# Strassen pairs for 24 of 32 down products of layer 1's MLP

## The chip, the cores and the metric

One Trainium2 chip, of which this kernel uses one core. The metric is the device time of one execution in microseconds. The core's engines run side by side, each with its own instructions in a fixed order: TensorE (PE) multiplies matrices, VectorE (DVE), ScalarE (ACT) and GpSimd (POOL) work element by element, SyncE (SP) issues the transfers between device memory and on-chip memory. They wait for one another through semaphores.

## The reference

A model of two layers over 1,040 tokens (16 learned ones ahead of 1,024 of the input), width 1,024, all in fp32. Each layer is a mixer (layer 0: stick-breaking attention beside an S5 state space; layer 1: a gated delta net) and an MLP, each with a norm before and after it and a residual. Only layer 1's MLP is touched:

```python
def sq_relu_mlp(h, w1, w2):
    return jnp.square(jax.nn.relu(h @ w1)) @ w2
...
        hn = rms_norm(hs, pre_mlp_norm[i])
        hs = hs + rms_norm(sq_relu_mlp(hn, mlp_w1[i], mlp_w2[i]), post_mlp_norm[i])
    return hs[:, N_META:]
```

`w1` is 1024 x 4096 and `w2` 4096 x 1024. Layer 1's MLP runs over the last 1,024 tokens alone, since only they are returned.

## The kernel before

Activations lie transposed: features on the 128 partitions, tokens along the row. A product in fp32 accuracy is three matmuls. Each operand is split into a high part (`split` and `weight` cast it on ACT into `hh` or `whi`) and a low part (what is left, a subtraction on DVE or POOL into `hl` or `wlo`); then high x high, high x low and low x high are added up in one PSUM bank. With 512 token columns that is three matmuls of 128 x 128 by 512.

The MLP (`mlp`) first makes the 4,096 hidden features in 32 tiles of 128 (up), then multiplies them with `w2` (down).

Up: tiles 0 to 5 plainly; tiles 6 to 31 in 13 pairs (`pair`) by Strassen's algorithm in Winograd's form, which multiplies 2 x 2 blocks with seven products in place of eight. The blocks are two hidden tiles by two halves of 512 tokens (tokens 16 to 527 and 528 to 1039). `ops` makes the weight sums of a pair on POOL (lines 451 to 459) and its seven split operands (line 440). Each product is 12 matmuls, and DVE adds the results up (line 487). `block` applies the square ReLU: on DVE a `scalar_tensor_tensor` with the row scale `rb` (line 491), on ACT the square (line 415). Each of the four finished blocks is stored by SP to a buffer in device memory, `hd` (line 416).

Down: `down([2g, 2g+1])` for 14 groups of two hidden tiles, then `down([28, 29, 30, 31], True)`, whose chunks are 384, 384 and 256 columns and with which the norm and the output go. `hidden(k)` loads one tile of activations (`hr`, or `wraw` for the first four), splits it, the low part on POOL (line 229). `weight` loads 128 x 1024 of `w2` into `wraw`, casts on ACT (line 163), makes the low part on POOL (line 166). For each of eight output tiles and two halves PE adds up both hidden tiles (six matmuls, lines 176 to 178), and DVE copies (line 552) or adds (line 554) the bank to `acc`.

The order of work on each engine is that in which the code is written, unless a scheduler of the framework moves it: instructions of one engine are put in order ahead of time, by when it expects operands and buffers. Buffers are rings: `wraw` has two tiles, `whi` and `wlo` four each, `slot` shares 33 tiles among many names. A write into a ring's tile waits until the last reader of what lay there is done.

Of the kernel before, what the change touches and what calls it, by code (L numbers as in the profile page):

```python
# [11 lines left out]
F32 = mybir.dt.float32  # L12
F32R = mybir.dt.float32r
BF16 = mybir.dt.bfloat16
I32 = mybir.dt.int32
AF = mybir.ActivationFunctionType
# [30 lines left out]
def f(ap):  # L47
    return ap.bitcast(F32)


class Net:
# [349 lines left out]
    def mlp(self, layer, st, hs_d, chunks, gpre, ahead=None):  # L401

        nc = self.nc
        w1, w2 = self.io["w1"], self.io["w2"]
        hd = self.dr.tile([128, 32, NT], F32, tag="hd%d" % layer, name="hd", bufs=1)
        hid = {}
        t0, h = (0, 520) if layer == 0 else (16, 512)
        half = ((0, 260), (260, 260)) if layer == 0 else ((0, 512),)
        wide = chunks if layer == 0 else CH4
# [3 lines left out]
        def put(m, o, n, x):  # L413

            nc.scalar.activation(x[:, :n], x[:, :n], AF.Square)
            nc.sync.dma_start(hd[:, m, o:o + n], x[:, :n])
# [13 lines left out]
        bank = cycle((self.mm, self.tr, self.mm, self.tr, self.mm, self.tr, self.ax))  # L430
# [12 lines left out]
        def ops(ma, mb):  # L443

            ra, rb = self.raw(), self.raw()
            nc.sync.dma_start(ra[:, :1024], w1[layer, ma])
            nc.sync.dma_start(rb[:, :1024], w1[layer, mb])
            a11, a12, a21, a22 = ra[:, :512], ra[:, 512:1024], rb[:, :512], rb[:, 512:1024]
            S = [self.sp.tile([128, 520], F32, tag="sS", name="sS", bufs=4)[:, :512] for _ in range(4)]
            o = [operand(a11)]  # L450
            nc.gpsimd.tensor_add(S[0], a21, a22)
            nc.gpsimd.tensor_sub(S[1], S[0], a11)
            o.append(operand(S[1]))
            o.append(operand(a12))
            nc.gpsimd.tensor_sub(S[2], a11, a21)
            o.append(operand(S[2]))
            o.append(operand(a22))
            o.append(operand(S[0]))
            nc.gpsimd.tensor_sub(S[3], a12, S[1])
            o.append(operand(S[3]))  # L460
            return o

        def pair(ma, mb, T):

            A11, S2, A12, S3, A22, S1, S4 = ops(ma, mb)
            B11 = lambda k: (st["hi"][k][:, t0:t0 + h], st["lo"][k][:, t0:t0 + h])
            B21 = lambda k: (st["hi"][k + 4][:, t0:t0 + h], st["lo"][k + 4][:, t0:t0 + h])
            B22 = lambda k: (st["hi"][k + 4][:, t0 + h:t0 + 2 * h], st["lo"][k + 4][:, t0 + h:t0 + 2 * h])
            T1, T3 = (lambda k: tuple(x[:, :h] for x in T[k][0])), (lambda k: tuple(x[:, h:2 * h] for x in T[k][0]))
            T4, T2 = (lambda k: tuple(x[:, :h] for x in T[k][1])), (lambda k: tuple(x[:, h:2 * h] for x in T[k][1]))  # L470

            def product(A, B, then):
                for c, (o, n) in enumerate(half):
                    pt = next(bank)()[:, :n]
                    for i in range(4):
                        wh, wl = (w[:, i * 128:(i + 1) * 128] for w in A)
                        bh, bl = B(i)
                        nc.tensor.matmul(pt, wh, bh[:, o:o + n], start=i == 0, stop=False)  # L478
                        nc.tensor.matmul(pt, wh, bl[:, o:o + n], start=False, stop=False)  # L479
                        nc.tensor.matmul(pt, wl, bh[:, o:o + n], start=False, stop=i == 3)  # L480
                    then(c, o, n, pt)

            P, U, R, Q = {}, {}, {}, {}

            def total(x, name, n, *ab):
                x = self.tmp(name) if x is None else x
                nc.vector.tensor_add(x[:, :n], *ab)
                return x

            def block(m, o, n, x):  # L490
                nc.vector.scalar_tensor_tensor(x[:, :n], x[:, :n], 0.0, st["rb"][:, o:o + n], op0=ALU.max, op1=ALU.mult)
                put(m, o, n, x)

            def p1(c, o, n, pt):
                P[c] = self.tmp("p1")
                nc.scalar.copy(P[c][:, :n], pt)

            def p2(c, o, n, pt):
                block(ma, t0 + o, n, total(P[c], "", n, pt, P[c][:, :n]))

            def p6(c, o, n, pt):
                U[c] = total(None, "u2", n, pt, P[c][:, :n])

            def p7(c, o, n, pt):
                R[c] = total(None, "u3", n, pt, U[c][:, :n])

            def p4(c, o, n, pt):
                block(mb, t0 + o, n, total(None, "c21", n, pt, R[c][:, :n]))

            def p5(c, o, n, pt):  # L510
                Q[c] = total(U[c], "", n, pt, U[c][:, :n])
                block(mb, t0 + h + o, n, total(R[c], "", n, pt, R[c][:, :n]))

            def p3(c, o, n, pt):
                block(ma, t0 + h + o, n, total(Q[c], "", n, pt, Q[c][:, :n]))

            product(A11, B11, p1)
            product(S2, T2, p6)
            product(A12, B21, p2)
            product(S3, T3, p7)  # L520
            product(A22, T4, p4)
            product(S1, T1, p5)
            product(S4, B22, p3)

        def hidden(k):

            raw = self.raw() if k < 4 else self.slot("hr")
            hi, lo = self.slot("hh", F32R), self.slot("hl", F32R)
            nc.sync.dma_start(raw[:, t0:NT], hd[:, k, t0:NT])
            self.split(hi[:, t0:NT], lo[:, t0:NT], raw[:, t0:NT], lo_eng=nc.gpsimd)  # L530
            hid[k] = (hi, lo)

        def down(ks, last=False):
            first = ks[0] == 0
            for k in ks:
                hidden(k)
            W = {k: self.weight(w2[layer, k], act=True) for k in ks}
            out, hook, ch = None, None, wide
            if last:
                ch = chunks  # L540
                if ahead is None:
                    ch = CH3
                if ahead is not None:
                    ahead()
                ssq = self.slot("ssq_o")
                reuse = [t for k in ks for t in hid[k]]
                *out, hook = self.residual(acc, ssq, reuse, G_POSTMLP + 8 * layer, hs_d, gpre, ch)

            def ev(m, c, pt):
                o, n = ch[c]  # L550
                if first:
                    nc.vector.tensor_copy(acc[m][:, o:o + n], pt)
                else:
                    nc.vector.tensor_add(acc[m][:, o:o + n], pt, acc[m][:, o:o + n])  # L554
                if last:
                    self.sq_acc(ssq, m, m == 0, acc[m][:, o:o + n], o, n)

            self.gemm(range(8), ks, lambda m, k: tuple(w[:, m * 128:(m + 1) * 128] for w in W[k]), lambda k: hid[k], ch, "c" if last else "m", ev, hook, None if last else six)
            for k in ks:
                del hid[k]  # L560
            return out
# [4 lines left out]
            up([m], "m")  # L566
        for m in range(UPC, 32, 2):
            pair(m, m + 1, T)
        acc = [self.slot("acc") for _ in range(8)]
        for g in range(14):  # L570
            down([2 * g, 2 * g + 1])
        return down([28, 29, 30, 31], True)


    def exp_exact(self, out, x):
# [1248 lines left out]


NSLOT, NTMP, AHEAD, UPC = 33, 10, 4, 6
ROW, RP, R0 = 1, 5, 2
FA, FB = 14, 14
RM = 4
# [315 lines left out]
```

## Time and profile before

| | |
|---|---|
| median of 3 runs | 2947.3 us (2946.3 to 2951.14) |
| the profiled execution | 2945.58 us |
| its span, first to last instruction | 2943.5 us |
| mean granted TensorE clock | 0.944 |
| TensorE busy in the span | 2767.2 us (94%), 16488 instructions recorded |
| VectorE busy | 1752.0 us (60%) |
| POOL busy | 1305.4 us (44%) |
| ScalarE busy | 1063.4 us (36%) |

Times in the trace count from the span's start. Layer 1's up pairs lie at about 2293 to 2564 us, the first down matmul at 2564.29 us, the last group of four from about 2873 us. In a row of a stage stand the stretch, its length, then for each engine busy microseconds and in brackets the instructions, then the granted clock (1.00 is full), the mean share of the DMA engines that were busy, and what they moved. In a row of the order of time stand start, length, engine, line, operation, and in square brackets how long the engine had been idle and who ended that.

### The profile page before, as it was taken

Reading aid. Unit: us, or ns where it says so; the run is one execution under the profiler, and the core shown is the slowest. Engines: PE = TensorE matmul, PEld = TensorE weight load, DVE = VectorE, ACT = ScalarE, POOL = GpSimd, SP = SyncE. Lnnn points to the kernel's source line nnn. Section 1 sums busy time; section 2 is a strip of 40 time slices with the busy share of each in tenths; the row PEclk is TensorE's granted clock in tenths of the full one; section 3 lists DMA queues with packets and bytes.
Section 4 is the critical chain, followed back from the end, with each engine's and each line's share of the span. In section 5 each row is a group of like instructions: output and inputs, shape, how many; then the busy total and the mean of one; then the engine's idle time right before and its main releaser. Section 6 shows DMA issues by size and latency. Waiting matters only on the chain. (4 is left out here: it accounts for less than half of the span.)

```text
span 2943.5 us, 44168 instructions
## 1 busy us (share of the span) xinstructions
PE 2767.2 (94%) x16488; PEld 2505.5 (85%) x16488; DVE 1752.0 (60%) x3107; ACT 1063.4 (36%) x2108; POOL 1305.4 (44%) x942
## 2 busy tenths in 40 slices
PE   7899999899999999999897978999998999999997
PEld 7689667788999999999886977899898888888887
DVE  8642768666755555555746896544538545444445
ACT  4111656554533332110446322443435433322101
POOL 5552324325577766342522123111135777664423
PEclk9989667889999999999998988999999999999998
DMA  3435212124433343221426667444334333442322
GB/s 129 157 122 157 80 57 80 48 87 167 133 112 114 111 146 136 95 80 54 135 90 214 198 204 230 126 139 141 121 105 153 118 113 104 135 155 94 107 88 70
DMA packets 209766, 360.99 MB, mean 123 GB/s; under 512 B 45488, under 2 KB 131200, under 8 KB 209552
## 3 DMA queue, kind: packets, MB, share of 16 engines
q1 hardware_dynamic: 205664, 353.49, 37.2%
q10 hardware_dynamic: 3888, 4.69, 0.4%
q8 instruction: 130, 2.13, 0.3%
q14 instruction: 84, 0.69, 0.1%
HBM read 247.07 MB, written 111.03 MB: 122 GB/s over the span
## 5 line engine op out<-in xcount | busy, mean ns | idle before, releaser
L166 POOL TENSOR_TENSOR wlo<-wraw,whi 128x1024 fp32r<-128x1024 f32 x129 | 315.2, 2456 | 764.6 <-ACT whi L163 272.7
L176 PE MATMUL mm<-ahi,whi 128*128 128x344 f32 (+2 forms) x1200 | 418.0, 349 | 41.3 <-DVE cx L1333 28.8
L178 PE MATMUL mm<-ahi,wlo 128*128 128x344 f32 (+2 forms) x1200 | 400.3, 334 | 2.3 <-DVE wlo L166 2.3
L177 PE MATMUL mm<-hl,whi 128*128 128x352 f32 (+4 forms) x1136 | 388.0, 342 | 0.0
L554 DVE TENSOR_TENSOR acc<-mm,acc 128x344 f32<-128x344 f32 (+4 forms) x308 | 177.3, 576 | 179.1 <-PE mm L178 179.1
L176 PEld LDWEIGHTS mm<-ahi,whi 128*128 128x128 f32 x1200 | 235.6, 196 | 49.6 <-DVE cx L1333 30.3
L178 PE MATMUL mm<-hh,wlo 128*128 128x352 f32 (+4 forms) x752 | 260.4, 347 | 5.0 <-POOL wlo L166 5.0
L176 PE MATMUL mm<-hh,whi 128*128 128x352 f32 (+4 forms) x752 | 260.2, 346 | 0.6 <-DVE acc L554 0.6
L178 PEld LDWEIGHTS mm<-ahi,wlo 128*128 128x128 f32 x1200 | 235.5, 196 | 4.3 <-DVE wlo L166 3.2
L554 DVE TENSOR_TENSOR acc<-tr,acc 128x344 f32<-128x344 f32 (+2 forms) x260 | 152.9, 588 | 139.7 <-PE tr L178 139.7
L177 PEld LDWEIGHTS mm<-hl,whi 128*128 128x128 f32 x1136 | 218.1, 192 | 11.2 <-issue 0.4
L163 ACT CAST whi<-wraw 128x1024 fp32r<-128x1024 f32 x77 | 77.6, 1045 | 351.7 <-PE tr L177 326.9
L178 PE MATMUL tr<-hh,wlo 128*128 128x512 f32 (+2 forms) x560 | 196.1, 350 | 0.0
L177 PE MATMUL tr<-hl,whi 128*128 128x512 f32 (+2 forms) x560 | 195.9, 350 | 0.0
L176 PE MATMUL tr<-hh,whi 128*128 128x512 f32 (+2 forms) x560 | 195.8, 350 | 0.0
L229 POOL TENSOR_TENSOR hl<-hr,hh 128x1040 fp32r<-128x1040 f32 (+1 forms) x56 | 135.6, 2429 | 78.0 <-ACT hh L228 62.3
L178 PEld LDWEIGHTS mm<-hh,wlo 128*128 128x128 f32 x752 | 143.1, 191 | 16.5 <-POOL wlo L166 6.2
L176 PEld LDWEIGHTS mm<-hh,whi 128*128 128x128 f32 x752 | 143.0, 190 | 10.9 <-DVE acc L554 0.9
L440 POOL TENSOR_TENSOR wlo<-sS,whi 128x512 fp32r<-128x512 f32 x104 | 143.4, 1381 | 14.1 <-ACT whi L439 14.0
L366 POOL TENSOR_TENSOR ssq_o<-ssq_o,sq 128x344 f32<-128x344 f32 (+4 forms) x84 | 93.9, 1117 | 79.8 <-ACT sq L365 79.3
L177 PE MATMUL mm<-hh,whi 128*128 128x344 f32 (+2 forms) x384 | 128.6, 335 | 0.0
L244 POOL TENSOR_TENSOR ssq<-ssq,sq 128x344 f32<-128x344 f32 (+2 forms) x84 | 90.6, 1079 | 84.9 <-ACT sq L243 76.8
(528 smaller groups left out, 7788.0 us busy)
## 6 DMA issues: line engine op xcount, KB each, us to landing
wraw<-w SPq DMA_DIRECT2D x128, 512.0 KB, 3.6
wraw<-wino SPq DMA_DIRECT2D x32, 512.0 KB, 5.2
hr<-hd SPq DMA_DIRECT2D x28, 520.0 KB, 5.6
hr<-hd SPq DMA_DIRECT2D x28, 512.0 KB, 4.5
dm<-dmd SPq DMA_DIRECT2D x16, 520.0 KB, 5.1
hsd<-hs SPq DMA_DIRECT2D x48, 172.0 KB, 1.9
hd<-u SPq DMA_DIRECT2D x52, 130.0 KB, 2.1
hd<-u SPq DMA_DIRECT2D x26, 256.0 KB, 2.0
```

The source lines that it names most:

```text
L163: nc.scalar.copy(hi[:, :n], raw[:, :n])
L166: (nc.vector if fast else nc.gpsimd).tensor_sub(lo[:, :n], raw[:, :n], f(hi[:, :n]))
L176: nc.tensor.matmul(pt, wh, h[:, o:o + n], start=i == 0, stop=False)
L177: nc.tensor.matmul(pt, wh, l[:, o:o + n], start=False, stop=False)
L178: nc.tensor.matmul(pt, wl, h[:, o:o + n], start=False, stop=i == len(kts) - 1)
L229: (lo_eng or nc.vector).tensor_sub(lo, src, f(hi))
L244: nc.gpsimd.tensor_add(st["ssq"][:, o:o + n], st["ssq"][:, o:o + n], sq[:, :n])
L366: nc.gpsimd.tensor_add(ssq[:, o:o + n], ssq[:, o:o + n], sq[:, :n])
L440: nc.gpsimd.tensor_sub(lo, src, f(hi))
L554: nc.vector.tensor_add(acc[m][:, o:o + n], pt, acc[m][:, o:o + n])
```

## The change

In layer 1 (`SD = (1,)`), hidden tiles 6 to 29 (`ND = 12` pairs) go through the down product in six groups of two pairs, by Strassen's algorithm as well: the blocks are now two hidden tiles by two token halves on one side, and two hidden tiles by two halves of the 1,024 output features on the other.

In the up pairs DVE makes four sums of the finished activation blocks (`sums`), and SP stores seven blocks per pair to a new buffer `ht` in place of four to `hd`.

`down_pairs(g, X)` goes through seven products, b = 0, 2, 4, 5, 3, 1, 6. For each it loads the activation blocks of two pairs into a raw weight tile (`raw()`, line 589), splits them with the low part on DVE (line 229), and multiplies by a weight block of both pairs: the quarters of `w2` are loaded in halves of 256 KB (`w2r`, line 568), and POOL makes the sums, S1 in a tile of its own (line 574) and three differences in place (line 579). The cast is on ACT (line 594), the low weights on POOL (line 595). Each product is 24 matmuls, four PSUM banks, which DVE copies (line 609, first group) or adds (line 611) to the seven sums `X`. `down([0, 1], X=X)` starts `acc` from its products and four of those sums (line 650), `combine(X)` adds the rest on DVE and POOL (lines 618 to 624), then follow `down([2, 3])` and `down([4, 5, 30, 31], True)`. On TensorE 14,788 rows become 14,644.

```diff
+SD, ND = (1,), 12
...
             def block(m, o, n, x):
                 nc.vector.scalar_tensor_tensor(x[:, :n], x[:, :n], 0.0, st["rb"][:, o:o + n], op0=ALU.max, op1=ALU.mult)
-                put(m, o, n, x)
+                if not seven:
+                    put(m, o, n, x)
+                    return
+                nc.scalar.activation(x[:, :n], x[:, :n], AF.Square)
...
+            def sums(o, n):
+
+                a, b, c, d = (H[k + (o,)][:, :n] for k in ((0, 0), (0, 1), (1, 0), (1, 1)))
+                ta, tb, tc = self.tmp("ta"), self.tmp("tb"), self.tmp("tc")
+                nc.vector.tensor_sub(ta[:, :n], b, a)
+                nc.vector.tensor_sub(b, d, b)
+                nc.vector.tensor_sub(tb[:, :n], d, ta[:, :n])
+                nc.vector.tensor_sub(tc[:, :n], c, tb[:, :n])
+                for i, x in ((5, ta), (3, H[0, 1, o]), (1, tb), (4, tc)):
+                    store(i, o, n, x)
...
+        def down_pairs(g, X):
+
+            kk = [UPC + 4 * g, UPC + 4 * g + 2]
+            v = lambda t: t[:, :1024]
+            R = {}
+
+            def load(i, k):
+                r = R[i, k] = self.slot("w2r")
+                for p in range(2):
+                    nc.sync.dma_start(r[:, p * 512:p * 512 + 512], w2[layer, kk[p] + k, :, i * 512:i * 512 + 512])
+                return r
+
+            def s1():
+                load(1, 0)
+                S1 = self.slot("w2s")
+                nc.gpsimd.tensor_add(v(S1), v(R[1, 0]), v(R[1, 1]))
+                R[2] = S1
+                return S1
+
+            def less(to, x, y):
+                nc.gpsimd.tensor_sub(v(to), v(x), v(y))
+                return to
+
+            steps = (
+                (0, lambda: load(0, 0)), (2, lambda: load(0, 1)), (4, lambda: load(1, 1)), (5, s1),
+                (3, lambda: less(R[1, 0], R[0, 0], R[1, 0])), (1, lambda: less(R[0, 0], R[2], R[0, 0])),
+                (6, lambda: less(R[0, 1], R[0, 1], R[0, 0])),
+            )
+            for b, make in steps:
+                raw, hi, lo = self.raw(), self.slot("hh", F32R), self.slot("hl", F32R)
+                nc.sync.dma_start(raw[:, :2 * h].rearrange("p (j t) -> p j t", j=2), ht[:, b, 2 * g:2 * g + 2, :h])
+                src = make()
+                self.split(hi[:, :2 * h], lo[:, :2 * h], raw[:, :2 * h])
+                whi = self.sb.tile([128, 1024], F32R, tag="whi", name="whi", bufs=4)
+                wlo = self.sb.tile([128, 1024], F32R, tag="wlo", name="wlo", bufs=4)
+                nc.scalar.copy(whi, v(src))
+                nc.gpsimd.tensor_sub(wlo, v(src), f(whi))
+                for m in range(4):
...
+                        if g == 0:
+                            nc.vector.tensor_copy(x, pt)
+                        else:
+                            nc.vector.tensor_add(x, pt, x)
+
+        def combine(X):
+
+            for m in range(4):
...
+                nc.vector.tensor_add(x6, x1, x6)
+                nc.gpsimd.tensor_add(acc[m][:, left], x1, acc[m][:, left])
+                nc.vector.tensor_add(x7, x6, x7)
+                nc.vector.tensor_add(x6, x5, x6)
+                nc.gpsimd.tensor_add(acc[m + 4][:, left], x7, acc[m + 4][:, left])
+                nc.gpsimd.tensor_add(acc[m + 4][:, right], x7, acc[m + 4][:, right])
+                nc.vector.tensor_add(acc[m][:, right], x6, acc[m][:, right])
...
+        X = None
+        if layer in SD:
+            X = {}
+            for g in range(ND // 2):
+                down_pairs(g, X)
         acc = [self.slot("acc") for _ in range(8)]
-        for g in range(14):
-            down([2 * g, 2 * g + 1])
-        return down([28, 29, 30, 31], True)
+        rest = [k for k in range(32) if X is None or not UPC <= k < UPC + 2 * ND]
+        down(rest[:2], X=X)
+        if X is not None:
+            combine(X)
+        for i in range(2, len(rest) - 4, 2):
+            down(rest[i:i + 2])
+        return down(rest[-4:], True)
```

What the change moves, at three places. First SP's transfers at the seam from up to down. A name before the arrow is what is written; the four stores of the last pair are those of `p1`, `c21`, `u3` and `u2` to `hd`. Before, with loads of hidden tiles (`wraw` from `hd`, later `hr`) and of `w2`:

```order
L416 DMA hd_22288<-u2_24718 128x512
L156 DMA wraw_24974<-w2 128x1024
L156 DMA wraw_24980<-w2 128x1024
L529 DMA wraw_25114<-hd_22288 128x1024
L416 DMA hd_22288<-p1_24852 128x512
L529 DMA wraw_25120<-hd_22288 128x1024
L416 DMA hd_22288<-c21_24914 128x512
L416 DMA hd_22288<-u3_24899 128x512
L416 DMA hd_22288<-u2_24867 128x512
L156 DMA wraw_25126<-w2 128x1024
L156 DMA wraw_25132<-w2 128x1024
L529 DMA hr_25266<-hd_22288 128x1024
```

Now; `wraw` from `ht` are the activations of blocks 5, 3 and 1 (those of 0, 2 and 4 stand further ahead); `w2r_25126`, `w2r_25173` and `w2r_25220` are the quarters for blocks 2 and 4 and for S1:

```order
L417 DMA hd_22288<-p1_24973 128x512
L417 DMA hd_22288<-c21_25035 128x512
L417 DMA hd_22288<-u3_25020 128x512
L417 DMA hd_22288<-u2_24988 128x512
L568 DMA w2r_25126<-w2 128x512 x2
L589 DMA wraw_25216<-ht_22289 128x2x512
L568 DMA w2r_25173<-w2 128x512 x2
L589 DMA wraw_25265<-ht_22289 128x2x512
L568 DMA w2r_25220<-w2 128x512 x2
L589 DMA wraw_25310<-ht_22289 128x2x512
```

The weights of the second block now stand behind the last store, and each later quarter behind an activation load into one of the two `wraw` tiles. Before, the weights of the first group of two hidden tiles stood ahead of the last pair's stores.

Then POOL from the last up operand on. Before, the low parts of activations (line 229) and weights (line 166) of the first groups:

```order
L440 TENSOR_TENSOR wlo_24836<-sS_24812,whi_24835 128x512
L229 TENSOR_TENSOR hl_24964<-wraw_24962,hh_24963 128x1024
L229 TENSOR_TENSOR hl_24970<-wraw_24968,hh_24969 128x1024
L166 TENSOR_TENSOR wlo_24977<-wraw_24974,whi_24976 128x1024
L166 TENSOR_TENSOR wlo_24983<-wraw_24980,whi_24982 128x1024
L229 TENSOR_TENSOR hl_25116<-wraw_25114,hh_25115 128x1024
L229 TENSOR_TENSOR hl_25122<-wraw_25120,hh_25121 128x1024
L166 TENSOR_TENSOR wlo_25129<-wraw_25126,whi_25128 128x1024
L166 TENSOR_TENSOR wlo_25135<-wraw_25132,whi_25134 128x1024
```

Now, with the weights of the blocks in the order b = 0, 2, 4, 5, 3, 1, 6:

```order
L441 TENSOR_TENSOR wlo_24957<-sS_24933,whi_24956 128x512
L595 TENSOR_TENSOR wlo_25085<-w2r_25079,whi_25084 128x1024
L595 TENSOR_TENSOR wlo_25132<-w2r_25126,whi_25131 128x1024
L595 TENSOR_TENSOR wlo_25179<-w2r_25173,whi_25178 128x1024
L574 TENSOR_TENSOR w2s_25223<-w2r_25220,w2r_25173 128x1024
L579 TENSOR_TENSOR w2r_25220<-w2r_25079,w2r_25220 128x1024
L579 TENSOR_TENSOR w2r_25079<-w2s_25223,w2r_25079 128x1024
L595 TENSOR_TENSOR wlo_25228<-w2s_25223,whi_25227 128x1024
L595 TENSOR_TENSOR wlo_25273<-w2r_25220,whi_25272 128x1024
L595 TENSOR_TENSOR wlo_25318<-w2r_25079,whi_25317 128x1024
L579 TENSOR_TENSOR w2r_25126<-w2r_25126,w2r_25079 128x1024
L595 TENSOR_TENSOR wlo_25363<-w2r_25126,whi_25362 128x1024
```

The low activations have left POOL (DVE has them), and ahead of the fourth block's low weights three sums of weights have come in.

Last POOL at the end of the new part, where `acc` and `X` are combined (lines 619, 622 and 623; those of line 622 wait for DVE's line 650) ahead of `down([2, 3])`. Before, in the middle of the down groups, as these stand everywhere:

```order
L229 TENSOR_TENSOR hl_25268<-hr_25266,hh_25267 128x1024
L166 TENSOR_TENSOR wlo_25281<-wraw_25278,whi_25280 128x1024
L166 TENSOR_TENSOR wlo_25287<-wraw_25284,whi_25286 128x1024
L229 TENSOR_TENSOR hl_25274<-hr_25272,hh_25273 128x1024
L229 TENSOR_TENSOR hl_25420<-hr_25418,hh_25419 128x1024
L229 TENSOR_TENSOR hl_25426<-hr_25424,hh_25425 128x1024
```

Now:

```order
L622 TENSOR_TENSOR acc_26959<-x_25276,acc_26959 128x512
L623 TENSOR_TENSOR acc_26959<-x_25276,acc_26959 128x512
L622 TENSOR_TENSOR acc_26960<-x_25276,acc_26960 128x512
L623 TENSOR_TENSOR acc_26960<-x_25276,acc_26960 128x512
L622 TENSOR_TENSOR acc_26961<-x_25293,acc_26961 128x512
L623 TENSOR_TENSOR acc_26961<-x_25293,acc_26961 128x512
L622 TENSOR_TENSOR acc_26962<-x_25293,acc_26962 128x512
L229 TENSOR_TENSOR hl_27145<-wraw_27143,hh_27144 128x1024
L623 TENSOR_TENSOR acc_26962<-x_25293,acc_26962 128x512
L229 TENSOR_TENSOR hl_27151<-wraw_27149,hh_27150 128x1024
L166 TENSOR_TENSOR wlo_27158<-wraw_27155,whi_27157 128x1024
L166 TENSOR_TENSOR wlo_27164<-wraw_27161,whi_27163 128x1024
```

The splits for k = 2 and 3, the last two `hl` and `wlo`, stand behind the additions to `acc`, the first of them behind all but the last one.

More of the change, by code (lines that the diff above doesn't have):

```diff
@@ L406, in mlp @@
         hid = {}
+        ht = self.dr.tile([128, 7, ND, 520], F32, tag="ht%d" % layer, name="ht", bufs=1) if layer in SD else None
         t0, h = (0, 520) if layer == 0 else (16, 512)
@@ L483, in pair @@
             P, U, R, Q = {}, {}, {}, {}
+            seven = layer in SD and (ma - UPC) // 2 < ND
+            H = {}
             def total(x, name, n, *ab):
@@ L491, in block, with store @@
                 nc.vector.scalar_tensor_tensor(x[:, :n], x[:, :n], 0.0, st["rb"][:, o:o + n], op0=ALU.max, op1=ALU.mult)
-                put(m, o, n, x)
+                if not seven:
+                    put(m, o, n, x)
+                    return
+                nc.scalar.activation(x[:, :n], x[:, :n], AF.Square)
+                i, r = (m - ma, int(o >= t0 + h))
+                H[i, r, o - t0 - r * h] = x
+                if (i, r) != (0, 1):
+                    store({(0, 0): 0, (1, 0): 2, (1, 1): 6}[i, r], o - t0 - r * h, n, x)
+            def store(b, o, n, x):
+                nc.sync.dma_start(ht[:, b, (ma - UPC) // 2, o:o + n], x[:, :n])
+            def sums(o, n):
[7 more added lines that the diff above has]
+                    store(i, o, n, x)
             def p1(c, o, n, pt):
@@ L515, in p3 @@
                 block(ma, t0 + h + o, n, total(Q[c], "", n, pt, Q[c][:, :n]))
+                if seven:
+                    sums(o, n)
             product(A11, B11, p1)
@@ L531, in hidden @@
             hid[k] = (hi, lo)
-        def down(ks, last=False):
+        def down_pairs(g, X):
[31 more added lines that the diff above has]
+                for m in range(4):
+                    if (b, m // 2) not in X:
+                        X[b, m // 2] = self.slot("x")
+                    for o, n in half:
+                        pt = next(bank)()[:, :n]
+                        for p in range(2):
+                            wh, wl = (w[:, p * 512 + m * 128:p * 512 + m * 128 + 128] for w in (whi, wlo))
+                            bh, bl = (x[:, p * h + o:p * h + o + n] for x in (hi, lo))
+                            nc.tensor.matmul(pt, wh, bh, start=p == 0, stop=False)
+                            nc.tensor.matmul(pt, wh, bl, start=False, stop=False)
+                            nc.tensor.matmul(pt, wl, bh, start=False, stop=p == 1)
+                        x = X[b, m // 2][:, m % 2 * h + o:m % 2 * h + o + n]
+                        if g == 0:
+                            nc.vector.tensor_copy(x, pt)
+                        else:
+                            nc.vector.tensor_add(x, pt, x)
@@ new lines, in combine @@
+        def combine(X):
+            for m in range(4):
+                x1, x6, x2, x7, x4, x5, x3 = (X[b, m // 2][:, m % 2 * h:m % 2 * h + h] for b in range(7))
+                left, right = slice(t0, t0 + h), slice(t0 + h, t0 + 2 * h)
+                nc.vector.tensor_add(x6, x1, x6)
[5 more added lines that the diff above has]
+                nc.vector.tensor_add(acc[m][:, right], x6, acc[m][:, right])
@@ L534, in down @@
+        def down(ks, last=False, X=None):
             first = ks[0] == 0
@@ L550, in ev @@
                 o, n = ch[c]
-                if first:
+                if first and X is not None:
+                    for r in range(2):
+                        a, e = max(o, t0 + r * h), min(o + n, t0 + r * h + h)
+                        if a < e:
+                            x = X[{(0, 0): 2, (0, 1): 6, (1, 0): 4, (1, 1): 5}[m // 4, r], m % 4 // 2]
+                            i = a - t0 - r * h + m % 2 * h
+                            nc.vector.tensor_add(acc[m][:, a:e], pt[:, a - o:e - o], x[:, i:i + e - a])
+                elif first:
                     nc.vector.tensor_copy(acc[m][:, o:o + n], pt)
```

## The prediction

> **What bounds the kernel now.** I read first the stages of layer 1's MLP (time, then busy time and, in brackets, instructions of PE, PEld, DVE, ACT and POOL, then granted clock, DMA share, GB/s). 2293 to 2544 holds the up pairs, 2564.3 to 2850 down products.
>
> ```profile
> 2293.00:2544.00 251.00, 251.00 (x1121) 206.73 (x1121) 125.28 (x147) 93.12 (x163) 194.67 (x143) 1.00 0.34 109
> 2564.30:2850.00 285.70, 285.70 (x1235) 231.58 (x1234) 143.08 (x207) 57.05 (x58) 133.56 (x56) 1.00 0.31 105
> 2350.00:2400.00 50.00, 50.00 (x217) 40.53 (x216) 23.40 (x27) 17.48 (x31) 39.61 (x31) 1.00 0.39 121
> ```
>
> TensorE is busy for every microsecond of both, at full clock; the others have slack, POOL least in the pairs (194.67 of 251, 15.0 us in each of 13 pairs). So here a matmul taken away is time gained, as long as nobody becomes late. One 512-column matmul takes 50/217 = 0.2304 us.
>
> Then the seam between up and down, in order of time (start, us, engine, line):
>
> ```profile
> 2564.06 0.40 PE L480 MATMUL ax<-ahi,wlo 128*128 128x512 f32 x1
> 2564.29 0.40 PE L176 MATMUL mm<-hh,whi 128*128 128x512 f32 x1
> 2564.40 2.52 SPq L416 DMA_DIRECT2D hd<-u  x2
> 2564.49 0.69 DVE L487 TENSOR_TENSOR u<-ax,u 128x512 f32<-128x512 f32 x1 [0.78 <-PE ax L480]
> 2565.22 0.69 DVE L491 SCALAR_TENSOR_TENSOR u<-u,rb 128x512 f32<-128x512 f32 x1
> 2565.94 0.63 ACT L415 ACTIVATE u<-u 128x512 f32<-128x512 f32 x1 [1.57 <-DVE u L491]
> ```
>
> PE goes from the last up product to the first down product without a gap. The last block is stored some 2.6 us after PE began on down, and SP stands on that store until then: whatever stands behind it in SP's order starts 2.6 us into down.
>
> **What is gained.** 14,788 PE rows become 14,644: 144 matmuls of 512 columns less, 144 x 0.2304 = 33.2 us, all on the path.
>
> **What the new part costs.** Each block of `down_pairs` needs, in a chain, an activation load, two 256-KB weight halves, a cast, and on POOL the low weights, for three blocks with a weight sum before it. Prices (ns: min/median/max; DMA: KB, us to landing; of the four DMA rows the last is of the crowded seam):
>
> ```profile
> L163 ACT CAST whi<-wraw x32: 1041/1047/1052, 2553.0 to 2875.8; 128x1024 fp32r<-128x1024 f32 x32
> L166 POOL TENSOR_TENSOR wlo<-wraw,whi x33: 2364/2407/2888, 2288.9 to 2878.3; 128x1024 fp32r<-128x1024 f32 x33
> L166 DVE TENSOR_TENSOR wlo<-wraw,whi x13: 1207/1221/2691, 8.8 to 2241.7; 128x1024 fp32r<-128x1024 f32 x13
> L229 POOL TENSOR_TENSOR hl<-hr,hh x28: 2392/2406/2442, 2579.6 to 2797.7; 128x1024 fp32r<-128x1024 f32 x28
> L554 DVE TENSOR_TENSOR acc<-mm,acc x128: 409/692/693, 2588.0 to 2929.9; 128x512 f32<-128x512 f32 x104, 128x384 f32<-128x384 f32 x16, 128x256 f32<-128x256 f32 x8
> L440 POOL TENSOR_TENSOR wlo<-sS,whi x52: 1278/1302/1786, 2306.0 to 2545.5; 128x512 fp32r<-128x512 f32 x52
> wraw<-w SPq DMA_DIRECT2D x57, 512.0 KB, 3.4
> hr<-hd SPq DMA_DIRECT2D x28, 512.0 KB, 4.5
> ta<-hsd SPq DMA_DIRECT2D x2, 256.0 KB, 3.5
> hr<-hd SPq DMA_DIRECT2D x11, 512.0 KB, 6.2
> ```
>
> A cast is 1.05, POOL's subtraction or sum of 1024 columns 2.41, the same on DVE 1.22, an evacuation 0.69. I count from the first down matmul (0); a block is 24 matmuls, 5.53 us, and its third matmul already needs the low weights.
>
> *First group.* The orders shown ahead put the weights of block 2 behind the last store: issue 2.6, landed 6.6 (4.0, between the 3.5 alone and 6.2 crowded), cast 7.7, low part 10.1. Block 0 ends at 5.53, and PE can begin five matmuls of the next; stall 3.4, block 2 ends 14.5. Block 4's weights stand behind an activation load whose tile waits for a DVE subtraction, itself behind block 0's third evacuation (6.3); its low parts are complete at 16.4: stall 1.7, end 21.7. Block 5 is the worst: SP holds its second weight half behind the activations of block 3, whose tile is freed at 16.4; landed 21.7; then POOL in order makes S1, two differences and only then the low weights: 4 x 2.41 and 1.2 lost to DVE's subtraction = 32.5; stall 9.9. The three blocks left cost 2.1. In before POOL did nothing between whole weights and low weights here, and loads ran ahead.
>
> *Second group.* Its first weights stand behind a load that waits for the low activations of group one's last block: 3.0; its S1 chain once more, 5.2; the block behind it 1.7. From the third group on the loads have run ahead: POOL 11 operations x 2.41 = 26.5, and DVE's 7 x 1.22 against 38.7 us of PE per group. Cost nothing, covered by PE; without cover 35.1 of 38.7 still fits.
>
> Run-in, sum: 3.4 + 1.7 + 9.9 + 2.1 + 3.0 + 5.2 + 1.7 = 27.0. Low 12: single-load prices, no collisions, second group free (2.8 for block 2, 7.8 for block 5, 1 after; block 5 can't do better, as its half waits for block 2's third evacuation). High 35: all loads at 6.2.
>
> *Combine and the second plain pair.* `down([0,1],X)` evacuates with the same count of DVE operations as before. POOL then has twelve 512-column adds (1.30), the last ones behind the evacuations of the last tile; behind them in POOL's order stand the low activations of k=2 and 3. With PE done with k=0,1 at T: last evacuation and add T+0.8, low activations 3.2; the raw tile is free only then, weights land 6.7 (3.4), cast 7.9, low weights behind the second activations 10.3 and 14.0 for k=3. PE's sixth matmul already needs k=3: stall 14.0 - 5 x 0.23 = 12.9 (low 11.9). In before the weights of the next pair had been split during the last one. DVE's 16 combining operations run under this stall and cost nothing; without it they would be 16 x 0.69 = 11 us in front of evacuations.
>
> *Clock.* Idle stretches of TensorE and what came after them:
>
> ```profile
> 31.68 0.66 PE L177 MATMUL mm<-alo,whi 128*128 128x352 f32 x1 [4.37 <-DVE alo L232]
> 31.68:37.50 5.82, 5.82 (x20) 5.82 (x21) 5.72 (x22) 0.22 (x1) 1.67 (x2) 0.50 0.00 0
> 1723.90 0.66 PE L176 MATMUL mm<-ahi,whi 128*128 128x352 f32 x1 [13.04 <-DVE cx L1333]
> 1723.90:1727.10 3.20, 3.20 (x11) 3.20 (x12) 3.20 (x5) 0.00 (x0) 0.00 (x0) 0.50 0.97 385
> 1727.10:1730.00 2.90, 2.90 (x20) 2.86 (x18) 2.90 (x4) 1.01 (x1) 0.00 (x0) 1.00 0.70 133
> ```
>
> After 4.37 us idle the clock is 0.50 for 5.82 us, after 13.04 idle for 3.20 and then 1.00: half of that is lost, 1.6 to 2.9. Three of the stalls are long enough (9.9, 5.2, 12.9). Behind the first two stand further stalls that partly take the loss up; I take 3.2 in all, ends 1.6 and 8.7. [...]
>
> *The pairs.* Twelve of 13 pairs get four DVE operations of 512 columns and seven stores instead of four. DVE has room (125.28 of 251), SP's stores are 36 x 256 KB more at a DMA share of 0.34: nothing, covered; but DVE's operations on two SBUF operands collide with POOL:
>
> ```profile
> L491 DVE SCALAR_TENSOR_TENSOR p<-p,rb x13: 691/1294/3750, 2320.2 to 2554.1; 128x512 f32<-128x512 f32 x13
> L491 DVE SCALAR_TENSOR_TENSOR c<-c,rb x13: 692/1164/1751, 2325.8 to 2559.6; 128x512 f32<-128x512 f32 x13
> 2505.89 1.33 POOL L451 TENSOR_TENSOR sS<-wraw 128x512 f32<-128x512 f32 x1 [1.92 <-DMA wraw<-w]
> 2524.01 1.29 POOL L451 TENSOR_TENSOR sS<-wraw 128x512 f32<-128x512 f32 x1 [3.76 <-DMA wraw<-w]
> ```
>
> The same operation takes from 0.69 to 3.75 us, while the evacuation row above, which reads PSUM, stays at 0.69. If POOL loses the 4 x 0.69 = 2.8 us of each pair, it has 15.0 + 2.8 = 17.8 of 19.3 and its turn of 1.9 to 3.8 us on the weight load no longer fits wholly. I take 0 to 5, point 0, as the row of POOL's share is the nearest.
>
> *The last group* is the same code: in before
>
> ```profile
> PE mm L178 <- POOL wlo L166: 2.5, 2, 1.3
> ```
>
> and I add 1 for its later loads.
>
> Sum: -33.2 + 27.0 + 12.9 + 3.2 + 1 = +10.9. The profiled execution took 2945.6 us, 1.7 under the median of the runs; on the median's basis 2947.3 + 10.9 = **2958**. Lowest of all terms: -33.2 + 12 + 11.9 + 1.6 = -7.7, 2940; highest: -33.2 + 35 + 14 + 8.7 + 2 + 5 = +31.5, 2979.
>
> **Rivals.** No change means within 0.2% (5.9 us), about what a measurement here can tell.
>
> A, the forecast: run-in of 20 or more and the combine stall; 2948 to 2965. Chance 0.56.
>
> B, the other side: the first group's chain is at its floor and the second is covered. Loads land as single ones do (3.4), so the second group's three stalls of 9.9 go. For it: SP then only waits on DVE, which is half idle. Against: 11 landings at the old seam took 6.2. Run-in 12, time 2940; it decides "faster" once run-in lies under 13.8 (33.2 - 11.9 - 1.6 - 5.9). Chance 0.15.
>
> C: the pairs become bound by the operand port that DVE and POOL share. POOL's period is 15.0 + 2.8 + 3.8 = 21.6 against 19.3: 2.3 x 12 = 27 us, less a lead of some 21 that POOL has at the start and that is then missing in the run-in; about 15 more, 2973. For it: the 3.75; against: medians of 1.2 to 1.3. Chance 0.14. [...]
>
> D: groups three to six do not run ahead, because the two raw tiles only free after DVE's subtraction; a stall of 3 us each, 2970. Against: 7 blocks of lookahead. Chance 0.10.
>
> The rest (0.05) is unknown. Range from B's upper part to C: 2942 to 2976. Faster 0.15 (B and a little of A's edge); within 0.2%: 0.20 (A's lower part, 2948 to 2953, and run-ins near 15); slower 0.65.
>
> **What would show it.** In the changed kernel's waits of PE: POOL's low weights (line 595) at the first two groups, the longest near 10 us in front of block 5; then one of about 13 us split over POOL's line 166 and ACT's cast, after the twelve adds; a clock of 0.50 for 3 us behind each. Groups three to six should be 38.7 us each, without waits. Wrong, if the SP queue turns out to run ahead of DVE's subtractions, if low weights are delayed by port waits throughout, or if the pairs take more than 251 us for 13.

## The result, and the profile after

The changed kernel takes 2967.5 us (median of 4 runs, 2965.1 to 2969.1), before 2946.8: ratio 1.0067, 95% interval 1.0055 to 1.0079, slower by some 20 us. The forecast was 2958, slower. The ratios below leave out a single execution, one of the twelve of first_group_on_act, which took 14,357 us beside 2939 to 2958 of the others.

The stages, in the columns of the prediction's first rows; up pairs, down without the last group, last group. Before:

```profile
2290.00:2564.29 274.29, 274.29 (x1228) 226.14 (x1227) 134.75 (x158) 102.85 (x176) 208.96 (x150) 1.00 0.36 116
2564.29:2873.00 308.71, 308.71 (x1334) 250.21 (x1333) 154.22 (x224) 59.05 (x60) 138.33 (x58) 1.00 0.33 114
2873.00:2943.50 70.50, 55.40 (x330) 52.08 (x328) 37.96 (x78) 14.30 (x29) 26.39 (x26) 0.89 0.17 60
```

After (the second row runs from the first down matmul, through the six Strassen groups, `combine` and `down([2,3])`, to the last group):

```profile
2290.00:2563.15 273.15, 273.15 (x1221) 225.00 (x1219) 178.94 (x207) 100.54 (x174) 205.95 (x147) 1.00 0.46 146
2563.15:2893.00 329.85, 295.13 (x1192) 232.79 (x1191) 210.77 (x257) 98.31 (x98) 226.06 (x91) 0.93 0.43 136
2893.00:2963.20 70.20, 54.66 (x329) 51.36 (x327) 37.62 (x78) 14.30 (x29) 26.52 (x26) 0.89 0.21 75
```

TensorE is still busy all through the up pairs, although DVE does 44 us more there, and the last group is as long as it was. The pairs' first and last products (line, number, ns min/median/max, first and last start), before and after:

```profile
L478 PE MATMUL mm<-ahi,whi x104: 389/393/396, 2311.0 to 2552.4; 128*128 128x512 f32 x104
L478 PE MATMUL ax<-ahi,whi x52: 393/396/398, 2327.7 to 2563.6; 128*128 128x512 f32 x52
```

```profile
L479 PE MATMUL mm<-ahi,whi x104: 389/393/396, 2309.8 to 2551.3; 128*128 128x512 f32 x104
L479 PE MATMUL ax<-ahi,whi x52: 393/396/398, 2326.5 to 2562.4; 128*128 128x512 f32 x52
```

From 2311.0 to 2563.6 and from 2309.8 to 2562.4: 252.6 us in both. DVE's multiplication by the row scale got slower beside the new subtractions, from 1.29 to 1.54 us in the median, but TensorE didn't wait for it:

```profile
L494 DVE SCALAR_TENSOR_TENSOR p<-p,rb x13: 692/1539/7942, 2319.1 to 2553.4; 128x512 f32<-128x512 f32 x13
```

All of the change lies in the middle row: 308.7 us became 329.9, with 144 matmuls less. Of the 329.85, TensorE idled 329.85 - 295.13 = 34.7 us. Its 1200 matmuls at 0.2304 us need 276.5; it was busy for 295.1, 18.6 more, nearly all of it for a slower clock (0.93 in the row, 1.00 before). 34.7 + 18.6 - 33.2 = 20.1; the two rows differ by 21.1, since at 308.71 / 1344 = 0.2297 us a matmul was a little cheaper in this stage before.

The order of time of TensorE shows where it idled (in square brackets; line 604 is high x high of `down_pairs`, 605 high x low, 606 low x high):

```profile
2570.75 0.50 PE L604 MATMUL mm<-hh,whi 128*128 128x512 f32 x1 [1.86 <-ACT whi L594]
2573.20 0.79 PE L606 MATMUL mm<-hh,wlo 128*128 128x512 f32 x1 [1.03 <-POOL wlo L595]
2579.71 0.50 PE L605 MATMUL tr<-hl,whi 128*128 128x512 f32 x1 [0.28 <-DVE hl L229]
2590.47 0.79 PE L604 MATMUL tr<-hh,whi 128*128 128x512 f32 x1 [5.19 <-ACT whi L594]
2596.56 0.79 PE L606 MATMUL tr<-hh,wlo 128*128 128x512 f32 x1 [4.02 <-POOL wlo L595]
2605.60 0.51 PE L604 MATMUL mm<-hh,whi 128*128 128x512 f32 x1 [2.58 <-ACT hh L228]
2608.18 0.79 PE L605 MATMUL mm<-hl,whi 128*128 128x512 f32 x1 [1.39 <-DVE hl L229]
2628.52 0.50 PE L604 MATMUL mm<-hh,whi 128*128 128x512 f32 x1 [1.64 <-ACT whi L594]
2631.63 0.80 PE L606 MATMUL mm<-hh,wlo 128*128 128x512 f32 x1 [1.69 <-POOL wlo L595]
2675.97 0.50 PE L604 MATMUL mm<-hh,whi 128*128 128x512 f32 x1 [0.81 <-DVE x L611]
2686.85 0.80 PE L604 MATMUL mm<-hh,whi 128*128 128x512 f32 x1 [3.65 <-DVE x L611]
...
2865.38 0.79 PE L176 MATMUL mm<-hh,whi 128*128 128x512 f32 x1 [7.47 <-ACT whi L163]
2867.81 0.80 PE L178 MATMUL mm<-hh,wlo 128*128 128x512 f32 x1 [1.21 <-POOL wlo L166]
2869.28 0.79 PE L176 MATMUL mm<-hh,whi 128*128 128x512 f32 x1 [0.67 <-ACT whi L163]
2871.72 0.80 PE L178 MATMUL mm<-hh,wlo 128*128 128x512 f32 x1 [1.22 <-POOL wlo L166]
```

The first group waits at blocks 2, 4, 5 and 3, the second at its first block, the third twice for DVE, and `down([2,3])` for its weights behind `combine`. Between the third group and `combine` there is nothing for 170 us. Ahead of the 3.65 us of the third group stand, on ACT and on DVE:

```profile
2683.30 1.04 ACT L228 CAST hh<-wraw 128x1024 fp32r<-128x1024 f32 x1 [9.04 <-POOL wlo L595]
2684.38 1.23 DVE L229 TENSOR_TENSOR hl<-wraw,hh 128x1024 fp32r<-128x1024 f32 x1 [5.14 <-ACT hh L228]
```

DVE's evacuations (line 611) follow behind this subtraction. POOL, for which ACT waits, came to the low weights only after three weight differences in a row (line 579; 2.4, 3.3 and 3.3 us).

In the rows of TensorE the second number, the matmul's length, is 0.79 where the clock is down. How long it is down, stretch by stretch:

```profile
2572.80:2576.00 3.20, 2.79 (x7) 2.22 (x8) 0.69 (x1) 1.22 (x2) 0.44 (x2) 0.50 0.34 129
2589.90:2599.95 10.05, 5.46 (x12) 3.87 (x13) 0.69 (x1) 2.61 (x3) 9.97 (x5) 0.50 0.02 9
2606.90:2613.40 6.50, 5.21 (x12) 4.13 (x13) 3.07 (x4) 1.04 (x1) 0.15 (x1) 0.50 0.28 81
2630.80:2637.35 6.55, 5.72 (x14) 4.48 (x14) 2.59 (x3) 3.14 (x3) 6.36 (x4) 0.50 0.64 235
2685.70:2692.10 6.40, 5.25 (x12) 4.13 (x13) 5.46 (x9) 2.00 (x2) 4.29 (x2) 0.50 0.64 183
2863.00:2876.00 13.00, 7.52 (x15) 4.71 (x16) 1.38 (x2) 5.02 (x5) 10.46 (x5) 0.50 0.60 216
```

Six stretches at 0.50, 31.95 us of busy TensorE, of which half, 16.0 us, is lost. The other 2.6 of the 18.6 us the trace doesn't put down to anything; the first matmul after a wait counts as 0.50 us of work even at full clock (at 2570.75, 2605.60 and 2675.97 us, where the granted clock reads 1.00).

### The profile page after: what moved, and what is told of

It reads as the page before. It is cut to its first block, busy times and chain, and to the rows that moved or that the text cites. A ratio compares the mean times of both kernels' runs of the same rounds, so it can differ in the third digit from the quotient of the medians.

```text
span 2963.2 us, 44229 instructions
## 1 busy us (share of the span) xinstructions
PE 2750.7 (93%) x16344; PEld 2484.2 (84%) x16344; DVE 1858.2 (63%) x3189; ACT 1100.3 (37%) x2144; POOL 1389.1 (47%) x972
## 5 line engine op out<-in xcount | busy, mean ns | idle before, releaser
L177 PE MATMUL mm<-hl,whi 128*128 128x344 f32 (+5 forms) x944 | 313.1, 332 | 0.0
L176 PE MATMUL mm<-hh,whi 128*128 128x344 f32 (+4 forms) x560 | 185.5, 331 | 8.7 <-ACT whi L163 8.1
L178 PE MATMUL mm<-hh,wlo 128*128 128x344 f32 (+4 forms) x560 | 185.4, 332 | 7.4 <-POOL wlo L166 7.4
L654 DVE TENSOR_TENSOR acc<-mm,acc 128x344 f32<-128x344 f32 (+4 forms) x212 | 111.0, 523 | 126.1 <-PE mm L178 126.1
L654 DVE TENSOR_TENSOR acc<-tr,acc 128x344 f32<-128x344 f32 (+1 forms) x164 | 86.5, 528 | 73.7 <-PE tr L178 73.7
L595 POOL TENSOR_TENSOR wlo<-w2r,whi 128x1024 fp32r<-128x1024 f32 x36 | 97.4, 2713 | 66.5 <-ACT whi L594 64.4
L177 PE MATMUL tr<-hl,whi 128*128 128x344 f32 (+1 forms) x368 | 120.9, 329 | 0.0
L178 PE MATMUL tr<-hh,wlo 128*128 128x344 f32 (+1 forms) x368 | 120.9, 329 | 0.0
L176 PE MATMUL tr<-hh,whi 128*128 128x344 f32 (+1 forms) x368 | 120.9, 328 | 0.0
L1106 DVE TENSOR_TENSOR_SCAN keep<-keep,cst 128x400 f32<-128x400 f32 (+5 forms) x72 | 95.7, 1342 | 39.2 <-ACT keep L1104 38.9
```

What stands on the lines that cost most here:

```text
L176: nc.tensor.matmul(pt, wh, h[:, o:o + n], start=i == 0, stop=False)
L177: nc.tensor.matmul(pt, wh, l[:, o:o + n], start=False, stop=False)
L178: nc.tensor.matmul(pt, wl, h[:, o:o + n], start=False, stop=i == len(kts) - 1)
L595: nc.gpsimd.tensor_sub(wlo, v(src), f(whi))
L1106: v.tensor_tensor_scan(kp[:n, 0:L][:, ::-1], kp[:n, 0:L][:, ::-1], self.one_row[:n, :L], 1.0, op0=ALU.mult, op1=ALU.mult)
```

## The experiments

The work ahead of the MLP is the same in all kernels, but its length varies from execution to execution by up to 18 us (the first down matmul stands at 2558 to 2576 us of the span). So kernels are compared by one more number: the time from the first down matmul to the end of the profiled span, called the rest. Before it is 379.2 us, in the changed kernel 400.1. Ratios are of whole runs to runs of before on the same chip. The rest is read in one execution of each kernel, and how far it varies between executions was not measured; by the ratios combine_on_dve saves 6.5 us, loads_ahead 15 and both_ahead 29, each uncertain by 6 to 7. eight_pairs and low_on_pool ran only once.

**combine_on_dve** takes POOL's additions out from in front of the splits:

```diff
-                nc.gpsimd.tensor_add(acc[m][:, left], x1, acc[m][:, left])
+                nc.vector.tensor_add(acc[m][:, left], x1, acc[m][:, left])
...
-                nc.gpsimd.tensor_add(acc[m + 4][:, left], x7, acc[m + 4][:, left])
-                nc.gpsimd.tensor_add(acc[m + 4][:, right], x7, acc[m + 4][:, right])
+                nc.vector.tensor_add(acc[m + 4][:, left], x7, acc[m + 4][:, left])
+                nc.vector.tensor_add(acc[m + 4][:, right], x7, acc[m + 4][:, right])
```

> The twelve additions of combine go from POOL to DVE, nothing else. Theory (POOL's additions stand in front of the splits of k=2 and 3; each wait costs itself and the half clock behind it): the waits of 7.5, 1.2, 0.7 and 1.2 us and about 4 us of half clock go, 15 us less than the changed kernel, 2952 to 2954. Rival 1 (the half clock only moves time that the next wait would have taken): 10 to 11 us less, about 2957. Rival 2 (the splits are late for another reason, or DVE is now the one that is late): under 4 us less, 2964 or more.

Rest 389.6, 10.5 less than the changed kernel; ratio to before 1.0045 (1.0029 to 1.0061). The waits of TensorE between 2820 us and the last group, who waits for whom, total, times, longest; first the changed kernel:

```profile
PE mm L176 <- ACT whi L163: 8.1, 2, 7.5
PE mm L178 <- POOL wlo L166: 2.4, 2, 1.2
```

then with the additions on DVE:

```profile
PE mm L176 <- DVE acc L650: 2.9, 1, 2.9
```

The wait for the weights is gone: POOL's additions were its cause. A shorter one has come, since now DVE is late with `acc`. The gain lies with rival 1's number, but the new wait of 2.9 us, with a half clock of its own behind it (matmuls of 0.63 us instead of 0.40 until 2863.7, 5.7 us from the wait's end), explains the missing 4.5 just as well; this run doesn't tell the two apart.

**loads_ahead** asks for the first group's weights early:

```diff
+            if g == 0:
+                for i, k in ((0, 0), (0, 1), (1, 1), (1, 0)):
+                    load(i, k)
             for b, make in steps:
```

(`load` returns a quarter that is there already.)

> The first group's four weight quarters are asked for ahead of its activations, so that they stand in front of the last pair's stores in SP's order. Theory (the first group waits for its weights, late behind stores and activation loads): the waits in front of blocks 2 and 5 (2.9 and 9.2 us) and most behind them go, with the half clock behind them, 20 to 28 us less than the changed kernel, 2940 to 2948. Rival (the two raw tiles and DVE's subtractions set the pace, the weights only come late with them): 8 us less or under, 2959 or more.

Rest 379.5, 20.6 less; ratio 1.0016 (0.9999 to 1.0033). That is the theory's number, at its low end; the 15 us by the ratios lie between theory and rival. The waits in front of `combine`:

```profile
PE mm L609 <- DVE x L616: 4.2, 2, 3.6
PE mm L610 <- DVE hl L229: 2.9, 2, 1.5
PE mm L611 <- POOL wlo L600: 2.5, 2, 1.7
PE mm L609 <- ACT whi L599: 1.6, 1, 1.6
PE mm L609 <- ACT hh L228: 1.3, 1, 1.3
PE tr L611 <- POOL wlo L600: 1.0, 1, 1.0
PE tr L610 <- DVE hl L229: 0.4, 1, 0.4
```

In sum 13.9 us, before the edit 24.1 (34.7 less the 10.6 at `combine`). The first group's waits for weights (2.9 at block 2 and 9.2 at block 5) are gone, and the clock no longer falls there (up to 2671 us, in the third group, no matmul takes over 0.50 us, where 0.79 stood): the order of the weights in SP's queue was their cause. What stays in the first group is 4.6 us, mostly for DVE's subtractions; the second group waits 5.1 for its weights, the third 4.2 for DVE.

**filled_waits** asks what the slow clock costs by itself:

```diff
+                fill({(0, 2): 10, (0, 5): 36, (0, 3): 16, (1, 0): 14, (2, 2): 18}.get((g, b), 0))
```

and 44 ahead of `down([2,3])`. The six numbers add up to 138 matmuls (31.8 us), not the 136 of the expectation.

> 136 matmuls of 512 columns whose results nobody reads are put in front of the blocks where TensorE waits (10, 36, 16, 14, 18 and 44), about 31 us of work for 34.7 us of waits; all else is as in the changed kernel. Theory (the half clock behind a wait is a cost of its own, 19.6 us in all): TensorE stays at full clock, and 12 to 19 us go, 2949 to 2956. Rival (what the half clock takes, the next wait would have taken anyway, since the chain of loads and splits sets the pace): 0 to 5 us less, 2963 to 2968. If the fillers come on top of the waits: 31 us more.

Rest 395.2, 4.8 less; ratio 1.0055 (1.0034 to 1.0076). The stage from the first down matmul to the last group:

```profile
2558.15:2882.20 324.05, 314.08 (x1330) 251.09 (x1329) 211.45 (x257) 98.08 (x98) 225.17 (x91) 0.99 0.42 138
```

The clock is 0.99 instead of 0.93. Idle are 324.05 - 314.08 = 10.0 us; busy 314.1 = 276.5 + 31.8 of fillers + 5.8 of slow clock. So 12.8 us of slow clock went, and the waits, filled or not, grew from 34.7 to 10.0 + 31.8 = 41.8. The fillers themselves didn't outlast a wait: behind each of the six places TensorE still waited, from 0.2 us (`down([2,3])`) to 2.0 (block 5). So the time lies in the rival's range, at its upper end: of the 12.8 us, 7.1 came back as waiting, as if TensorE now arrived earlier at blocks whose operands come no sooner. A little under half of what the slow clock takes (5.7 of 12.8) is then a cost of its own. By the ratios the saving is 3.5 us, uncertain by 7, so this share rests on one execution. The fillers also read the tiles of the block ahead and so hold them longer; whether that delays later casts was not tested.

**both_ahead** joins the first two edits.

> combine's additions on DVE and the first group's weights ahead of its activations, both edits together. Theory (two separate causes): the two savings add up, 35 to 43 us less than the changed kernel, 2925 to 2933, faster than before by 0.5 to 0.7%. Rival (one resource behind both): clearly less than the sum, 2945 or more.

Rest 370.0, 30.1 less than the changed kernel, against 10.5 + 20.6 = 31.1 for the two alone: they add up, as the theory has it, though the sum stays under the range expected, as the part of combine_on_dve does. Ratio to before 0.9969 (0.9948 to 0.9990): faster than before. The largest waits left:

```profile
PE mm L609 <- DVE x L616: 4.8, 1, 4.8
PE mm L176 <- DVE acc L655: 3.8, 2, 2.7
PE mm L610 <- DVE hl L229: 2.9, 2, 1.5
```

All three are DVE's now.

**plain_pair_first** gives the new part plain products as cover: `down([0,1])`, 96 matmuls, 22 us in the trace and not the 44 of the expectation.

```diff
+        down(rest[:2])
+        if layer in SD:
+            X = {}
+            for g in range(ND // 2):
+                down_pairs(g, X)
         for i in range(2, len(rest) - 4, 2):
             down(rest[i:i + 2])
+        if layer in SD:
+            combine(X)
```

(blocks 2, 4 and 6 go straight into `acc`, `combine` has 32 operations on DVE).

> down([0,1]) goes ahead of the Strassen groups, whose blocks 2, 4 and 6 then add straight into acc; combine comes after down([2,3]), on DVE, with 32 operations. Theory (the new part's chains lack only cover at its beginning; 44 us of plain products let loads and POOL run ahead): the waits of TensorE in the first groups go nearly all, as does that of combine; what is left is DVE's wait in the third group (4 to 5 us) and its half clock. From the first down matmul to the end 355 to 365 us (before 379.2, changed 400.1), faster than before by 0.5 to 0.8%. Rival (POOL or DVE bind the blocks throughout, the groups would wait later instead): 375 us or more.

Rest 387.0; ratio 1.0034 (1.0018 to 1.0050). The theory failed, and the time is in the rival's range. The largest waits from 2580 us on:

```profile
PE tr L604 <- DVE x L616: 10.9, 4, 3.5
PE tr L606 <- POOL wlo L595: 4.2, 2, 2.2
PE mm L604 <- ACT hh L228: 3.7, 1, 3.7
PE mm L604 <- DVE x L616: 3.1, 1, 3.1
```

The run-in did not vanish (about 12 us of waits in the first two groups, 19.7 in the changed kernel), and DVE's wait, which the changed kernel has in one group, is in four. The engines' order of time at the first of these:

```profile
2699.68 1.05 ACT L228 CAST hh<-wraw 128x1024 fp32r<-128x1024 f32 x1 [11.32 <-POOL wlo L595]
2700.76 1.22 DVE L229 TENSOR_TENSOR hl<-wraw,hh 128x1024 fp32r<-128x1024 f32 x1 [7.04 <-ACT hh L228]
2702.50 0.68 DVE L616 TENSOR_TENSOR x<-mm,x 128x512 f32<-128x512 f32 x1
```

DVE stands 7 us in front of a subtraction that waits for ACT's cast, which itself waited 11 us for POOL. An evacuation is queued behind it, and TensorE waits for its bank. It is the chain of the changed kernel's third group again: each engine takes its work in sequence, and one late operand holds what is behind it. Why the cast must wait for POOL is open. It writes one of the 33 tiles that `slot` shares, and in this kernel `acc` and `X` hold 16 of them during the groups, in the changed kernel 14; that tiles are short was not tested.

**eight_pairs** sets ND to 8.

> ND is 8 instead of 12: 16 of 32 down products go by Strassen, four groups instead of six. Theory (the cost is one of beginning and end, each pair gains 12 matmuls, 2.76 us): two groups less lose 11.1 us, from the first down matmul to the end 411 us (changed 400.1). Rival (each group costs its share, 54 us / 6 = 9 a group against a gain of 5.5): 393 us.

Rest 409.1, the theory's 411 and far from the rival's 393. TensorE's waits up to the last group are 35.7 us with four groups, 34.7 with six. So the cost lies in the first three groups and at the end of the new part and is paid once; each pair beyond gains.

**low_on_pool** gives the low activations back to POOL:

```diff
-                self.split(hi[:, :2 * h], lo[:, :2 * h], raw[:, :2 * h])
+                self.split(hi[:, :2 * h], lo[:, :2 * h], raw[:, :2 * h], lo_eng=nc.gpsimd)
```

> The low parts of the activations in down_pairs are made on POOL instead of DVE, as before's hidden does. Theory: POOL then has 18 operations of 2.41 us a group, 43.4 us against 38.7 of TensorE, and becomes the bound in all six groups: 410 to 440 us from the first down matmul to the end, with waits for POOL's low parts throughout. Rival (DVE's subtractions standing in front of its evacuations are what holds the raw tiles and the banks): 390 us or less.

Rest 420.4, and POOL is what binds (stage of the six groups, then the two largest waits):

```profile
2569.40:2845.00 275.60, 236.34 (x945) 181.75 (x944) 109.41 (x159) 86.05 (x87) 250.81 (x106) 0.95 0.39 126
PE tr L606 <- POOL wlo L595: 17.7, 9, 7.7
PE mm L606 <- POOL wlo L595: 9.8, 8, 1.5
```

POOL is busy for 250.8 of 275.6 us. That DVE makes the low parts in the changed kernel is right: on POOL they cost 20 us more.

**less_on_dve** and **first_group_on_act** try to take the rest from both_ahead: the first leaves the four additions of `x1` on POOL, the second also has ACT copy the first group's results.

```diff
-                            nc.vector.tensor_copy(x, pt)
+                            nc.scalar.copy(x, pt)
```

> As both_ahead, but four of combine's twelve additions (x1 to the left half of acc[0] to acc[3], which are ready early) stay on POOL; DVE has eight more than in the changed kernel. Theory (in both_ahead DVE is the one that is late at combine, 2.67 + 1.14 + 1.14 us): these waits shrink by 2 to 5 us, 365 to 368 us from the first down matmul to the end (both_ahead 370.0), 0.3 to 0.5% faster than before. Rival (POOL's additions collide with DVE's on the shared port): 370 to 374 us.

> As less_on_dve, and the first group's 28 results are copied out of PSUM by ACT instead of DVE, so that DVE's subtractions have no evacuation in front of them there. Theory (behind the loads, what is left of the run-in, 1.5 + 0.5 + 1.3 + 1.4 us, comes from subtractions queued behind evacuations on DVE): 3 to 5 us less than less_on_dve. Rival (ACT's casts now stand behind its copies, and weights and activations come later): equal or up to 8 us more.

less_on_dve: rest 369.2, 0.8 less than both_ahead, with a ratio of 0.9972 (0.9957 to 0.9988); no better than both_ahead by these numbers. DVE's waits at `combine` fell from 5.0 to 1.9, and one of 1.6 for POOL's low weights came. first_group_on_act: rest 381.0, 11.8 more, ratio 1.0001 (0.9982 to 1.0019): the rival's way, by the rest beyond its 8 us. TensorE's waits for ACT's casts up to the last group are 8.1 us, in less_on_dve 3.1, since the casts stand behind the copies; those for DVE's subtractions did not shrink (4.3 and 3.2).

## Why the prediction was right, and where not

The sign, the run-in of the first group and the wait at `combine` were right; the size was not, +10.9 us forecast and +20.7 measured. The 2967.5 us lie in the stated range of 2942 to 2976, but above the 2948 to 2965 of rival A, the forecast's own.

- *The gain*, 33.2 us: right. 1192 of 1200 matmuls are in the trace, and eight_pairs loses what the matmuls of two groups are worth (9.0 us in the rest against 11.1).
- *First group*: block 2 forecast 3.4, measured 1.86 + 1.03 = 2.9; block 4 1.7 and 0.3; block 5 9.9 and 5.19 + 4.02 = 9.2; the blocks behind it 2.1 and 2.58 + 1.39 = 4.0. POOL's sum S1 ahead of block 5 (line 574) took 3.32 us beside a subtraction of DVE's (at 2586.02 us) and 2.43 where none ran: 0.9 lost, where the step has 1.2. loads_ahead shows the cause for blocks 2 and 5, the weights behind the last store and behind activation loads; which of the two weighs more it doesn't tell.
- *Second group*: its first block 3.0 and 1.64 + 1.69 = 3.3. The S1 chain there (5.2) and the block behind it (1.7) did not wait at all, so that step failed by 6.9. Probably the second group's loads ran ahead while the first group stood still: in loads_ahead, where the first group waits 4.6 us and not 16.4, the same two places wait 1.05 and 0.79. That is still far from 6.9.
- *From the third group on* nothing was forecast, and there were 0.8 + 3.65 us for DVE. Rival D had named waits there of 3 us in each of four groups; they came in one, and not for D's reason, the raw tiles. The step added up POOL's and DVE's time per group (26.5 and 8.6 of 38.7 us) and not their order: POOL's weight differences come in a row, the cast waits 9.04 us behind them, and DVE's subtraction, with evacuations behind it, waits for the cast.
- *Run-in* in sum: 27.0 forecast, 24.1 measured with the third group. That these lie close is in part luck: 6.9 too much in the second group and 4.5 too little in the third. *Combine*: 12.9 and 10.6, caused by POOL's queue as the step says (combine_on_dve).
- *Clock*: 3.2 forecast as a net cost, ends 1.6 and 8.7; the slow clock took up to 18.6, 16.0 of it in the six stretches. This is the term that was mis-sized most. Three stalls were counted as long enough, by the row with 4.37 us idle, and the clock fell in six places. In each TensorE worked at 0.50 for 2.8 to 7.5 us, in four of the six for 5.2 to 5.7, near the longer of the two rows that were used (3.20 and 5.82); so two waits of 1.64 and 1.69 us cost as much clock here (5.72 us of work at 0.50) as two of 5.19 and 4.02 (5.46). That stalls behind take a part of the loss up was right. By filled_waits a little under half is net, about 8 us if that share holds for all 18.6 (an estimate). The rest of it, some 10 us, would be waits at full clock, 34.7 + 10 = 45 where 39.9 was forecast. Read so, clock and waits were each about 5 us too small, and neither alone makes the 9.8 us between forecast and result.
- *The pairs*: 0, and 0 it was; rival C, that DVE's and POOL's operations hold each other up until the pairs are bound by it, did not come (252.6 us in both). DVE's single operations did get longer: the multiplication by the row scale took 0.69 us in the 11 places where no operation of POOL's ran, and 7.94 beside six of them on end (2495.67 us; it ended 0.54 us after the last), while evacuations stayed at 0.69 beside POOL as well. There was room for it.
- *Last group*: 1 forecast, none measured (70.2 us and 70.5).
- *Rival B* (the run-in at its floor) is what loads_ahead makes of the kernel, and even so the ratio is 1.0016, since `combine` and the clock remain.

## What to carry to other kernels

Taking matmuls away from a stage that TensorE binds pays only what is left after the run-in of the new chain: count, at the seam, each load's place in the queue and what it stands behind, as here the weights behind the last store. A fixed cost of the first groups and the end (34.7 us of waits and 18.6 of slow clock here) calls for many repetitions, and here it came down by order, not by work: two edits that move no matmul and add no operation turned 20 us slower into 9 us faster. Adding up each engine's time per group doesn't show a wait: three weight differences in a row on POOL held a cast, the cast a subtraction, and the subtraction evacuations. Cover in front (plain_pair_first) did not take that wait away.

## What the runs showed of the hardware that was not expected

- The granted clock fell to 0.50 without a long wait. In the changed kernel it fell at two waits of 1.86 and 1.03 us with 1.4 us of work between them; in combine_on_dve behind a single wait of 2.85 us (it ends at 2857.97 us). At the second group's first block it fell in the changed kernel behind waits of 1.64 and 1.69 us with 1.4 us of work between them (0.50 from 2630.8 to 2637.35 us), but not in loads_ahead behind 1.57 and 1.70, again with 1.4 us between (at 2613.21 and 2616.35 us; the matmuls behind them take 0.39 to 0.40). So the lengths of the waits alone don't decide.
- At block 5 a second wait made the stretch at 0.50 longer, but hardly added to the loss, which is half of the work in it: 5.46 us of work (two waits, 10.05 us in all) against 5.25 in the third group (one wait of 3.65 us) and 5.82 us after 4.37 us idle in the kernel before. Only at `combine`, with four waits, it was more, 7.52 us.
